# One sum of FFN weights out of four per pair: by VectorE from SBUF instead of a load and an adding transfer

## The chip, the cores and the metric

The kernel runs on one core of a Trainium2 chip. The metric is the device time of one execution in microseconds. TensorE (PE in the profile) does the matrix products, VectorE (DVE) and ScalarE (ACT) the elementwise work, GpSimd (POOL) some small copies and the issue of the adding transfers, SyncE (SP) the issue of the plain loads.

## What is computed

One inference step of a decoder of two layers, for a prompt of 512 tokens and for 8 samples of 4 tokens (544 columns together), all in fp32, with 1024 channels. Layer 0 mixes with attention and a gated linear attention, layer 1 with a short convolution. Each layer ends with the same feed-forward block, and the change touches that block alone:

```python
def causal_dwconv(x, past, w):
    L = x.shape[1]
    xp = jnp.concatenate([past.astype(x.dtype), x], axis=1)
    y = w[0] * xp[:, 0:L]
    for i in range(1, CONV_W):
        y = y + w[i] * xp[:, i:i + L]
    return y, xp[:, L:]
...
def conv_ffn(h, w_up, conv_w, conv_b, w_down, past):
    u = h @ w_up
    uc, new = causal_dwconv(u, past, conv_w)
    gate, val = jnp.split(uc + conv_b, 2, axis=-1)
    return (jax.nn.gelu(gate, approximate=True) * val) @ w_down, new
```

`w_up` is 1024 x 5632 (2816 gate and 2816 value columns, 22 blocks of 128 each), `w_down` 2816 x 1024.

## The kernel before

**Units.** Weights go through the kernel in units of 128 partitions x 512 columns of fp32 (256 KB). A load puts a unit into a raw tile `wr` (11 buffers). `prepare` (line 193) then makes two tiles of it: `wh`, the unit rounded for TensorE, on ScalarE (line 199), and `wl`, the rest, on VectorE (line 203). The units of the whole program stand in one list, and `prepare` goes through it in order: the `wh` stand in that order on ScalarE ("hi"), the `wl` on VectorE ("lo"), the loads on SP's queue ("load"), the adding transfers on GpSimd's queue ("sum"). `mm3` (line 276) makes each product of three matmuls: high weights with high activations (line 280), with low ones (line 285), and low weights with high ones (line 287).

**The FFN.** `ffn_order` (line 453) mixes three kinds of step per layer: the first gate and value blocks one by one ("raw", "plain"), then 16 pairs (one gate block and its value block, `c` = 6 to 21), and "down" steps between them. The pairs come in groups of 3, 4, 4 and 5, with a down step behind each; behind the last five there are two.

**A pair.** `pair(c)` (line 1800) makes a gate block and a value block by a scheme with 7 products where the plain way takes 8. Each product is 4 units' columns by 272 tokens: 12 matmuls. The weights that it needs, in order: `a`, `s2`, `s1`, `b`, `s3`, `s4`, `d`. Of these `a`, `b`, `d` are plain weights and the other four are sums: `s1` of the gate's and the value's blocks, `s2` = `s1` plus `a`'s block, `s3` of two blocks, and `s4` = `s2` plus `b`'s block. `quads` (line 244) makes the sums in flight: one plain load, and an adding transfer on top of it, either from HBM (`rows`, line 256) or from another tile in SBUF (`more`, line 252). So a pair has 7 loads on SP and 4 adding transfers on GpSimd. All seven tiles are taken when the first is prepared; a product asks for its units 8 units ahead (line 344), about one pair.

**The results of a pair** lie in four PSUM banks out of five of `pg`. They are emptied by ScalarE (lines 1807, 1811, 1813) and VectorE: line 1809 (`u2`) must be through before the bank's next product, two products after its own; 1815 (`u3`), 1818 and 1819 (gate), 1822 to 1824 (value) follow. `conv` (line 1737) then makes the convolution (1741 ACT, 1742 and 1743 DVE), 1750 the product of gate and value, 527 its low part. GpSimd copies the edge rows of each block (line 1739) and opens the next `u` (1714, 1715). A down step empties 16 banks into `m` (line 607).

**Order.** The code is written product by product, and a scheduler sets each engine's order from its own model of time, within the chains named above. Each engine then runs strictly in that order.

Of the kernel before, what the change touches and what calls it, by code (L numbers as in the profile page):

```python
# [16 lines left out]
ALU = mybir.AluOpType  # L17
AX = mybir.AxisListType

P = 128  # L20
# [68 lines left out]
def tile_hybrid_step(  # L89
# [42 lines left out]
    V, S, G, PE = nc.vector, nc.scalar, nc.gpsimd, nc.tensor  # L132
# [12 lines left out]
    def nm(s):  # L145
        uid[0] += 1
        return f"{s}{uid[0]}"
# [42 lines left out]
    def raw_tile():  # L190
        return wpool.tile([P, UN], F32, tag="wr", name=nm("wr"), bufs=11)
# [23 lines left out]
    def in_turn(what, ins):  # L215

        if what in turn:
            behind(ins, turn[what])
        turn[what] = ins

    def unit(w, r0, c0, nkb=4):


        def load():
            wr = raw_tile()
            ins = nc.sync.dma_start(
                wr.rearrange("p (k c) -> p k c", k=nkb),
                w[r0 : r0 + nkb * P, c0 : c0 + UN // nkb].rearrange("(k p) c -> p k c", p=P),
            )
            in_turn("load", ins)  # L230
            return wr

        return load
# [10 lines left out]
    def quads(w, c1, c2):  # L244

        t = {}

        def load(k, r0, c0):
            t[k] = unit(w, r0, c0)()

        def more(k, src):
            in_turn("sum", G.dma_start(t[k], src, accum_op=ALU.add))  # L252

        def rows(k, r0, c0):
            src = w[r0 : r0 + 4 * P, c0 : c0 + P].rearrange("(k p) c -> p k c", p=P)
            in_turn("sum", G.dma_start(t[k].rearrange("p (k c) -> p k c", k=4), src, accum_op=ALU.add))  # L256

        def first():
            load("a", 0, c1)
            load("s1", 0, c2)  # L260
            rows("s1", 4 * P, c2)
            load("s2", 0, c1)
            more("s2", t["s1"])
            load("b", 4 * P, c1)
            load("s3", 0, c1)
            rows("s3", 0, c2)
            load("s4", 4 * P, c1)
            more("s4", t["s2"])
            load("d", 4 * P, c2)
            return t["a"]  # L270

        return [first] + [lambda k=k: t[k] for k in ("s2", "s1", "b", "s3", "s4", "d")]

    nxt = [0]

# [15 lines left out]
    def behind(ins, first):  # L291

        tc.add_manual_dep(
            ins.ins,
            first.ins.name,
            mybir.DependencyInfo(mybir.DependencyClass.NoSync, mybir.DependencyReason.DATA),
            reason="issue order",
        )
# [166 lines left out]
    def ffn_units(l):  # L465
        for kind, c, n in ffn_order():
            if kind == "down":
                units.extend(down(ffn_down[l], c * P, n))
            elif kind != "pair":
                for k in range(c, c + n):  # L470
                    units.extend(cols(ffn_up[l], k * P) + cols(ffn_up[l], F + k * P))
            else:
                units.extend(quads(ffn_up[l], c * P, F + c * P))
# [1559 lines left out]
```

## Time and profile before

| what | value |
|---|---|
| median of 3 runs | 1285.26 us (1282.33 to 1285.63) |
| profiled execution, its own time | 1285.74 us |
| its span from the first to the last instruction | 1283.9 us |
| PE busy | 1241.9 us, 97% |
| DVE busy | 959.5 us, 75% |
| ACT busy | 682.9 us, 53% |
| POOL busy | 383.1 us, 30% |
| plain loads (q1) / adding transfers and other GpSimd transfers (q0) | 132.17 MB / 34.74 MB |

The profile is of one execution. Busy time says how long an engine had an instruction running; the stretches (windows of 20 us and the like) tell where it was not. The granted clock of TensorE is given as a share of full speed, 1.00 being 2.4 GHz.

### The profile page before, as it was taken

To read this page: it belongs to the slowest core of one execution; us is meant where nothing else is said; L and a number is where in the kernel's file an instruction comes from. 1 tells how busy PE (TensorE), PEld (TensorE's weight loads), DVE (VectorE), ACT (ScalarE), POOL (GpSimd) and SP (SyncE) were. 2 spreads that over 40 slices of the span, in tenths; PEclk is the share of its full clock that TensorE was granted. 3 is DMA by queue.
4 is the path that set the end of the run, shared out by engine and by line. 5 is a ranking of instruction groups with operands and counts; after the bars stand their busy time and mean duration, and the time that the engine had idled before them with its cause. 6 is when DMAs were issued, how large, how long until landed. Compare 5 with 4: busy or idle time off the path is not lost.

```text
span 1283.9 us, 26460 instructions
## 1 busy us (share of the span) xinstructions
PE 1241.9 (97%) x9710; PEld 1204.6 (94%) x9710; DVE 959.5 (75%) x2054; ACT 682.9 (53%) x1489; POOL 383.1 (30%) x604
## 2 busy tenths in 40 slices
PE   8999998989999999999998999999999999999997
PEld 7999986888999999999998999998999999999897
DVE  7486477578979796977978655528897969697786
ACT  7554546755567373735645323335556646464553
POOL 4100210063443334343144000025243433242312
PEclk9999999999999999999999999999999999999999
DMA  8512220323568999999622322321467899999811
GB/s 256 137 50 66 84 87 1 102 67 99 115 134 203 196 212 195 213 195 216 172 75 58 107 85 84 96 75 42 124 128 161 189 210 210 206 208 192 197 41 70
DMA packets 311883, 171.97 MB, mean 134 GB/s; under 512 B 20829, under 2 KB 301882, under 8 KB 311738
## 3 DMA queue, kind: packets, MB, share of 16 engines
q1 hardware_dynamic: 262914, 132.17, 36.0%
q0 software_dynamic: 43456, 34.74, 18.8%
q10 hardware_dynamic: 5384, 3.38, 0.9%
q8 instruction: 76, 1.25, 0.4%
q14 instruction: 53, 0.43, 0.1%
HBM read 149.01 MB, written 5.47 MB: 120 GB/s over the span
## 4 chain that ended last, share of the span: by engine, by line
PE 81%; DVE 11%; ACT 3%; issue 2%; DMA 2%; POOL 0%; SPq 0%; POOLq 0%; DVEq 0%; ACTq 0%
PE pg L280 24%; PE pg L285 24%; PE pg L287 24%; DVE m L652 3%; DVE xres L656 2%; DVE xl L668 2%; PE ps L181 1%; DVE wl L203 1%; PE ps L1088 1%; PE ps L1363 1%; DMA wr<-ffn_up 1%; ACT h L538 1%; PE ps L1425 1%; PE ps L390 1%; DVE xl L527 1%
## 5 line engine op out<-in xcount | busy, mean ns | idle before, releaser
L199 ACT ACTIVATE wh<-wr 128x512 fp32r<-128x512 f32 x478 | 296.8, 629 | 400.5 <-PE pg L285 322.8
L280 PE MATMUL pg<-xh,wh 128*128 128x256 f32 (+2 forms) x1536 | 445.3, 292 | 10.2 <-DVE u L1819 6.0
L285 PE MATMUL pg<-xl,wh 128*128 128x256 f32 (+2 forms) x1536 | 442.6, 290 | 0.3 <-DVE xl L530 0.3
L287 PE MATMUL pg<-xh,wl 128*128 128x256 f32 (+2 forms) x1520 | 437.0, 290 | 0.0
L203 DVE TENSOR_TENSOR wl<-wr,wh 128x512 fp32r<-128x512 f32 x466 | 318.3, 693 | 128.3 <-ACT wh L199 116.8
L280 PEld LDWEIGHTS pg<-xh,wh 128*128 128x128 f32 x1536 | 290.3, 190 | 14.7 <-issue 8.5
L285 PEld LDWEIGHTS pg<-xl,wh 128*128 128x128 f32 x1536 | 291.7, 190 | 1.0 <-DVE xl L530 0.5
L287 PEld LDWEIGHTS pg<-xh,wl 128*128 128x128 f32 x1520 | 287.6, 190 | 0.5 <-issue 0.2
L285 PE MATMUL pg<-gl,wh 128*128 128x256 f32 (+1 forms) x704 | 201.0, 288 | 0.8 <-DVE gl L527 0.8
L287 PE MATMUL pg<-gh,wl 128*128 128x256 f32 (+1 forms) x704 | 200.1, 288 | 0.0
L280 PE MATMUL pg<-gh,wh 128*128 128x256 f32 (+1 forms) x704 | 197.2, 290 | 2.1 <-DVE m L607 1.7
L285 PEld LDWEIGHTS pg<-gl,wh 128*128 128x128 f32 x704 | 132.6, 188 | 1.2 <-DVE gl L527 1.2
L280 PEld LDWEIGHTS pg<-gh,wh 128*128 128x128 f32 x704 | 129.8, 188 | 3.2 <-DVE m L607 2.3
L287 PEld LDWEIGHTS pg<-gh,wl 128*128 128x128 f32 x704 | 132.3, 188 | 0.0
L256 POOL DMA_DIRECT2D wr<-ffn_up x64 | 92.6, 1446 | 113.1 <-DVE wl L203 52.5
L252 POOL DMA_DIRECT2D wr<-wr x64 | 59.2, 925 | 210.7 <-DMA wr<-ffn_up 44.7
L607 DVE TENSOR_TENSOR m<-m,pg 128x256 f32<-128x256 f32 (+1 forms) x176 | 72.0, 432 | 55.4 <-PE pg L287 55.0
L280 PE MATMUL pg<-qh,wh 128*128 128x272 f32 x384 | 110.2, 289 | 0.6 <-DVE h L1809 0.6
L287 PE MATMUL pg<-qh,wl 128*128 128x272 f32 x384 | 110.7, 289 | 0.0
L285 PE MATMUL pg<-ql,wh 128*128 128x272 f32 x384 | 110.6, 288 | 0.0
L1739 POOL COPY uc<-u 128x18 f32<-128x18 f32 x88 | 63.9, 894 | 80.7 <-DVE u L1819 37.4
L539 POOL TENSOR_TENSOR pss<-pss,h 128x256 f32<-128x256 f32 (+1 forms) x47 | 38.5, 818 | 120.9 <-ACT h L538 120.3
(327 smaller groups left out, 2203.0 us busy)
## 6 DMA issues: line engine op xcount, KB each, us to landing
wr<-ffn_up SPq DMA_DIRECT2D x272, 256.0 KB, 3.6
wr<-ffn_down SPq DMA_DIRECT2D x88, 256.0 KB, 3.4
wr<-ffn_up POOLq DMA_DIRECT2D x64, 256.0 KB, 5.9
wr<-wr POOLq DMA_DIRECT2D x64, 256.0 KB, 4.6
wr<-w_in_odd SPq DMA_DIRECT2D x48, 256.0 KB, 2.9
wr<-w_in_even SPq DMA_DIRECT2D x28, 256.0 KB, 4.2
wr<-w_out_odd SPq DMA_DIRECT2D x16, 256.0 KB, 2.5
xt<-x_prompt SPq DMA_DIRECT2D x8, 256.0 KB, 3.4
```

The lines of the kernel that those rows point to most:

```text
L199: ins = S.activation(wh, src, AF.Copy)
L203: ins = eng.tensor_tensor(wl, src, wh.bitcast(F32), ALU.subtract)
L252: in_turn("sum", G.dma_start(t[k], src, accum_op=ALU.add))
L256: in_turn("sum", G.dma_start(t[k].rearrange("p (k c) -> p k c", k=4), src, accum_op=ALU.add))
L280: ins = PE.matmul(ps[:, :n], lhsT=wh, rhs=xh[kb][:, sl], start=first, stop=False, skip_group_check=True)
L285: PE.matmul(ps[:, :n], lhsT=wh, rhs=xl[kb][:, sl], start=False, stop=last and packed, skip_group_check=True)
L287: PE.matmul(ps[:, :n], lhsT=wl, rhs=xh[kb][:, sl], start=False, stop=last, skip_group_check=True)
L539: ins = (V if c == NC - 1 else G).tensor_tensor(ss[:, sl], ss[:, sl], q[:, :n], ALU.add)
L607: V.tensor_tensor(self.m[m][:, sl], self.m[m][:, sl], ps[:, :n], ALU.add)
L652: chain(V.scalar_tensor_tensor(m, m, gcol(self.kind, self.l, c), self.bc[:, sl], ALU.mult, ALU.mult))
L656: chain(V.tensor_tensor(x, x, self.m[c][:, sl], ALU.add))
L1739: G.tensor_copy(ucv[:, :, :, c], u[:, TP : TP + 54].rearrange("p (g k) -> p g k", k=6)[:, :, 0:2])
```

## The change

`s4` is no longer loaded and added to in flight. When its turn comes, `last_sum` takes a raw tile and VectorE writes `b` + `s2` into it from the tiles in SBUF (line 272 of the changed kernel), in the chain "lo" of the `wl`. The other three sums stay.

```diff
             load("b", 4 * P, c1)
             load("s3", 0, c1)
             rows("s3", 0, c2)
-            load("s4", 4 * P, c1)
-            more("s4", t["s2"])
             load("d", 4 * P, c2)
             return t["a"]
 
-        return [first] + [lambda k=k: t[k] for k in ("s2", "s1", "b", "s3", "s4", "d")]
+        def last_sum():
+            wr = raw_tile()
+            in_turn("lo", V.tensor_tensor(wr, t["b"], t["s2"], ALU.add))
+            return wr
+
+        return [first] + [lambda k=k: t[k] for k in ("s2", "s1", "b", "s3")] + [last_sum, lambda: t["d"]]
```

With 16 pairs in each of two layers, 32 loads and 32 adding transfers go (SP's queue has 480 rows instead of 512, GpSimd 566 instead of 598) and 32 instructions come to VectorE (2021 instead of 1989). The scheduler sets the order anew around them; line numbers behind line 272 are 3 higher.

**GpSimd, the last two pairs of layer 0, before.** The tiles 8003, 8006, 8011, 8014 are `s1`, `s2`, `s3`, `s4` of pair 20, and 8175, 8178 `s1`, `s2` of pair 21.

```order
L256 DMA wr_8011<-ffn_up 128x4x128
L252 DMA wr_8014<-wr_8006 128x512
L256 DMA wr_8175<-ffn_up 128x4x128
L252 DMA wr_8178<-wr_8175 128x512
L1739 COPY uc_3682<-u_7889 128x18
L1739 COPY uc_3682<-u_7886 128x18
```

The same place of the changed kernel: 7997 is `s3` of pair 20, 8160 and 8163 are `s1` and `s2` of pair 21, and `u_8041`, `u_8044` belong to pair 19.

```order
L256 DMA wr_7997<-ffn_up 128x4x128
L1717 MEMSET u_8041 128x2
L1718 COPY u_8041<-stT_3138 128x8x2
L1717 MEMSET u_8044 128x2
L1718 COPY u_8044<-stT_3138 128x8x2
L256 DMA wr_8160<-ffn_up 128x4x128
L1742 COPY uc_3682<-u_8041 128x18
L1742 COPY uc_3682<-u_8044 128x18
L1717 MEMSET u_8212 128x2
L1718 COPY u_8212<-stT_3138 128x8x2
L1717 MEMSET u_8215 128x2
L1718 COPY u_8215<-stT_3138 128x8x2
```

The adding transfer into `s4` of pair 20 no longer stands ahead of `s1` of pair 21; that into `s2` of pair 21 (the row behind these) has moved behind the copies of pair 19's edge rows.

**VectorE, the same place, before.** `wl_8236` is the low part of `s2` of pair 21, `u_8058` and `u_8061` are gate and value of pair 19.

```order
L1815 TENSOR_TENSOR h_8057<-pg_8051,h_8054 128x272
L203 TENSOR_TENSOR wl_8236<-wr_8178,wh_8237 128x512
L1818 TENSOR_TENSOR u_8058<-pg_8052,h_8056 128x240
L1819 TENSOR_TENSOR u_8058<-pg_8052,h_8056 128x8x4
L1822 TENSOR_TENSOR u_8061<-h_8057,h_8055 128x240
L1823 TENSOR_TENSOR u_8061<-h_8057,h_8055 128x8x4
```

And of the changed kernel, where the low part of `s2` of pair 21 is `wl_8218`, and gate and value of pair 19 are `u_8041` and `u_8044`.

```order
L1827 TENSOR_TENSOR u_8044<-h_8040,pg_8036 128x272
L203 TENSOR_TENSOR wl_8117<-wr_8115,wh_8118 128x512
L203 TENSOR_TENSOR wl_8134<-wr_8000,wh_8135 128x512
L203 TENSOR_TENSOR wl_8173<-wr_8158,wh_8174 128x512
L1745 SCALAR_TENSOR_TENSOR y_8153<-u_8041,cw_3121,y_8153 128x560
L1812 TENSOR_TENSOR h_8210<-h_8208,pg_8205 128x272
L1745 SCALAR_TENSOR_TENSOR y_8193<-u_8044,cw_3121,y_8193 128x560
L1746 SCALAR_TENSOR_TENSOR y_8153<-u_8041,cw_3121,y_8153 128x560
L1746 SCALAR_TENSOR_TENSOR y_8193<-u_8044,cw_3121,y_8193 128x560
L1753 TENSOR_TENSOR y_8153<-y_8153,y_8193 128x560
L203 TENSOR_TENSOR wl_8218<-wr_8163,wh_8219 128x512
L203 TENSOR_TENSOR wl_8235<-wr_8160,wh_8236 128x512
```

The low part of `s2` of pair 21 has moved from ahead of the emptying of pair 19's banks to ten rows behind it.

**VectorE in a down step, changed kernel,** between groups of four pairs: the sum of the next group's first pair (`wr_5764`) stands between the emptyings of the down banks (line 610, before line 607).

```order
L610 TENSOR_TENSOR m_3674<-m_3674,pg_5548 128x288
L203 TENSOR_TENSOR wl_5760<-wr_5613,wh_5761 128x512
L272 TENSOR_TENSOR wr_5764<-wr_5611,wr_5608 128x512
L610 TENSOR_TENSOR m_3675<-m_3675,pg_5575 128x256
L610 TENSOR_TENSOR m_3675<-m_3675,pg_5576 128x288
```

Before, the same place has no sum.

```order
L607 TENSOR_TENSOR m_3674<-m_3674,pg_5551 128x288
L203 TENSOR_TENSOR wl_5766<-wr_5616,wh_5767 128x512
L607 TENSOR_TENSOR m_3675<-m_3675,pg_5578 128x256
L607 TENSOR_TENSOR m_3675<-m_3675,pg_5579 128x288
```

Of a group of four pairs, the sums of the first and the second stand in the down step ahead or right behind it, those of the third and fourth among the pairs.

## Rows read from the trace of the kernel before

**Rows 1.** Page, part 1: busy us, share of the span, instructions.

```profile
PE 1241.9 (97%) x9710; PEld 1204.6 (94%) x9710; DVE 959.5 (75%) x2054; ACT 682.9 (53%) x1489; POOL 383.1 (30%) x604
```

**Rows 2.** Stretches: start:end, us, PE, PEld, DVE, ACT, POOL busy, clock, DMA share, GB/s.

```profile
580.00:600.00 20.00, 20.00 (x162) 20.00 (x161) 18.26 (x37) 13.61 (x26) 6.59 (x11) 1.00 1.00 212
600.00:620.00 20.00, 17.18 (x125) 16.99 (x124) 13.42 (x27) 10.80 (x22) 5.05 (x15) 0.91 0.83 196
...
1200.00:1220.00 20.00, 16.85 (x120) 16.45 (x120) 14.94 (x30) 11.53 (x23) 6.71 (x15) 0.91 0.85 196
```

**Rows 3.** Chain that ended last, layer 0's last pairs: start us, us, what.

```profile
609.73 0.90 issue
...
612.54 0.50 PE pg L280
613.04 0.23 PE pg L285
...
616.44 0.12 PE pg L285
```

**Rows 4.** Timeline of ACT and DVE there: start, us, engine, line, operation, [idle before].

```profile
610.63 1.67 ACT L199 ACTIVATE wh<-wr 128x512 fp32r<-128x512 f32 x3 [7.09 <-PE pg L287]
...
611.29 0.69 DVE L203 TENSOR_TENSOR wl<-wr,wh 128x512 fp32r<-128x512 f32 x1 [6.36 <-ACT wh L199]
```

**Rows 5.** Timeline of POOL ahead of it, and one row of layer 1.

```profile
594.49 0.89 POOL L252 DMA_DIRECT2D wr<-wr  x1 [1.77 <-DVE wl L203]
595.20 1.52 POOL L256 DMA_DIRECT2D wr<-ffn_up  x1
603.12 0.88 POOL L252 DMA_DIRECT2D wr<-wr  x1 [6.40 <-DVE wl L203]
603.67 0.69 POOL L1739 COPY uc<-u 128x18 f32<-128x18 f32 x2
...
1203.67 2.34 POOL L1739 COPY uc<-u 128x18 f32<-128x18 f32 x2
```

**Rows 6.** DMA from 440 to 620 us: queues (packets, MB, share), issues (us to landing).

```profile
q1 hardware_dynamic: 50038, 25.36, 49.8%
q0 software_dynamic: 14256, 11.27, 44.5%
...
wr<-ffn_up POOLq DMA_DIRECT2D x21, 256.0 KB, 6.1
wr<-wr POOLq DMA_DIRECT2D x21, 256.0 KB, 4.7
```

**Rows 7.** Waits of SP's queue from 440 to 620 us: total, times, longest.

```profile
SPq L226 <- DMA wr<-wr: 42.1, 7, 10.5
```

**Rows 8.** Stretches of four pairs and of the down step behind them: DVE alone.

```profile
446.70:485.40 38.70, 35.32 (x72) 1.00 0.93 217
485.40:508.50 23.10, 16.43 (x32) 1.00 0.94 186
```

**Rows 9.** Timeline of DVE: a down step, and low parts back to back.

```profile
433.38 0.84 DVE L607 TENSOR_TENSOR m<-m,pg 128x256 f32<-128x256 f32 x2 [1.39 <-PE pg L287]
...
595.29 1.29 DVE L203 TENSOR_TENSOR wl<-wr,wh 128x512 fp32r<-128x512 f32 x2
```

**Rows 10.** Timeline of DVE: line 1809 in the four pairs from 442 us.

```profile
442.83 0.44 DVE L1809 TENSOR_TENSOR h<-h,pg 128x272 f32<-128x272 f32 x1 [0.29 <-PE pg L287]
...
465.63 0.43 DVE L1809 TENSOR_TENSOR h<-h,pg 128x272 f32<-128x272 f32 x1
```

**Rows 11.** Timeline of DVE at the end of these four pairs.

```profile
485.48 0.69 DVE L203 TENSOR_TENSOR wl<-wr,wh 128x512 fp32r<-128x512 f32 x1 [1.85 <-ACT wh L199]
486.23 1.55 DVE L1742 SCALAR_TENSOR_TENSOR y<-u,cw,y 128x560 f32<-128x560 f32 x2
...
489.12 1.48 DVE L607 TENSOR_TENSOR m<-m,pg 128x256 f32<-128x256 f32 x4
```

**Rows 12.** Chain that ended last at the same place.

```profile
489.20 0.34 DVE m L607
```

## The prediction

> **What bounds the kernel now.** I read the busy times first: TensorE has work for 97% of the span, VectorE for 75% [rows 1]. So only what takes idle time out of TensorE can gain, and an engine at 75% on average can still be full where it matters. Next the stretches of 20 us, to find where TensorE is not full: in undisturbed ones it runs 162 matmuls, 0.1235 us each, and in all the FFN there are two large holes, at the end of the last five pairs of either layer, with 125 and 120 matmuls and a granted clock of 0.91 [rows 2]. Small ones lie at the ends of the other groups of pairs. Then the chain at the first hole: TensorE ends a product at 609.7, starts the next at 612.54, and runs its matmuls at 0.23 us apart until 616, when they are 0.12 again [rows 3]; before it fell to that lower level (1.2 GHz against 2.4) it had been idle for the hole. What it waited for: ScalarE had sat idle for 7.09 us until it could round a unit, VectorE for 6.36 us behind that, with the emptying of a full bank queued behind this low part [rows 4]. By the order, the unit is `s2` of pair 21. Its sum was issued by GpSimd at 603.12, after a wait of 6.40 us for the adding transfer into `s1`, which itself had been issued at 595.20 [rows 5]. So the hole hangs on GpSimd's chain of adding transfers, beside DMA queues that are 94% taken from 440 to 620 us, 44.5 points by the adding queue although it moves less than half of the other's bytes [rows 6].
>
> **What goes.** Per pair one load and one of four adding transfers. In the stretch of rows 6 there are 42 adding transfers for 44.5 points, so a quarter of them gives back some 11 points, and ten loads of 256 KB, 2.6 MB of the plain queue's 25.36, some 5 more: the queues fall from 94% to about 78%. SP's queue waited 42.1 us in 7 waits on adding transfers that still read a tile [rows 7]; `d`'s buffer no longer waits for one that reads `s2`. On GpSimd the issue of the sum into `s4` goes: in the trace it waited 1.77 us and took 0.89 us ahead of the issue into `s1` of pair 21 [rows 5], which could have stood at 592.7 instead of 595.2. That alone brings the `s2` behind it 2.5 us forward. The transfers take 6.1 and 4.7 us from issue to landing [rows 6]; with queues at 78% I take each a microsecond shorter. So `s2` would be there some 4.5 us earlier, against a hole of 2.8 us [rows 3].
>
> The worth of the hole: TensorE is 162 - 125 = 37 matmuls short in layer 0 and 42 in layer 1, at 0.1235 us 4.6 and 5.2 us, 9.8 us together [rows 2]. From the other side: 20 - 17.18 and 20 - 16.85 us of idle are 6.0 us, and some 14 matmuls at 0.23 in place of 0.125 us in each hole are 1.5 us each [rows 3]: 9.0 us. I take 9.0, since a few matmul records may be missing.
>
> **What is added.** 32 sums on VectorE of 128x512. No row shows an addition of two raw tiles. The nearest is the low part, the same size from two tiles in SBUF: 0.69 us alone, two of them in 1.29 us [rows 4, 9], so 0.60 us of VectorE's time each when one follows another. 32 times 0.60 to 0.69 is 19 to 22 us, and the question is what hides it. The wait for data is nothing new, as `b` and `s2` have had their own low parts made ahead in the chain "lo". Behind the sum, ScalarE's rounding waits for VectorE and VectorE's low part for ScalarE; the order puts other rows between.
> - *In the down steps* VectorE is idle 1.39 us out of 3 behind each pair of emptied banks [rows 9], and 6.7 us of 23.1 in all [rows 8]. Of four sums of a group, two stand there or at its end: free.
> - *Among the pairs* VectorE is at 35.3 of 38.7 us [rows 8]; the other two sums (three in the groups of five) bring 1.2 to 1.4 us into 3.4 us of idle time, 1.85 us of which is itself a wait for a sum [rows 11]. Whether TensorE notices depends on line 1809: it has the two products between, 24 matmuls or 2.96 us. In the four pairs from 442 us it runs when TensorE lets it, at 442.83, and in the third pair at 465.63 [rows 10], where two pairs of 84 matmuls (10.4 us each) would put it at 463.6: 2.0 us late. In the new order I count VectorE's rows between two such lines: between the second and the third pair 7 low parts and a sum, between the third and the fourth 9 and a sum. With 0.60 to 0.65 us for these, 0.75 us for each step of the convolution [rows 11] and the rest as in the trace, that is some 9.5 and 13 us against 10.4 each: up to 2 us late, inside 2.96. I count nothing.
> - *At the group ends* TensorE waits 0.34 us today for `m` [rows 12], because VectorE comes late out of the pairs. The sums make it later by 1.2 us, the wait of 1.85 us for a sum [rows 11] goes. Six such ends (three per layer) can give from -0.5 us (today's stall gone) to +0.7 us (a sum exposed) each: -3 to +4 us. I take 0.
>
> **The sum.** The profiled execution took 1285.74 us, 1283.9 of it span; 1285.74 - 9.0 + 0 = 1276.7. The median of the runs is 0.5 us below that execution: 1276.3 us. Bounds of this case: -9.8 - 3 gives 1272.5, -9.0 + 4 with a microsecond of the hole left 1281.
>
> **Rivals.**
> *The wait stays on GpSimd.* The first three sums still go one after the other through its queue, and in the new order the issue into `s2` of pair 21 has moved behind the copies of pair 19's edge rows, which wait until VectorE has emptied pair 19's banks. From there: two copies, 0.7 us, four small ones, 0.6 us, issue and landing 4.7 us, 0.63 us for the rounding, nearly 7 us after pair 19's end; TensorE needs the unit one pair and one product after it, 11.9 us. That speaks against this rival; for it speaks that landing varies and that the copies wait for a late VectorE. It would keep the holes or half of them: 1281.5 to 1286, I say 1284.
> *GpSimd is held up by the new instructions.* The copy pair took 0.69 us once and 2.34 us in layer 1, where VectorE was running low parts [rows 5]. If the copies of two pairs ahead of `s2` stretch like that (twice 1.65 us) and VectorE is 2 us late besides, the margin of 4.9 us is used up, and a hole of up to 2 us without a fall of the clock stays in each layer: 1280. The Trainium skill says in "SBUF — State Buffer", section "SBUF: two separate sides", that VectorE and GpSimd share a pair of ports, which an instruction of VectorE with two inputs in SBUF holds against one of GpSimd that reads SBUF, for its whole length; the two copy rows agree with that. By it the time would be that of this rival, without it that of the forecast.
> *VectorE becomes the bound,* the case that ends slower. Place: line 1809 and the emptying into `m`. Price: the sums among the pairs, 9 or so per layer, each exposed at 0.65 us, 11.7 us, and the low parts come so late that the holes stay: 1297; with the holes gone 1288. It decides from the point where line 1809 is more than 2.96 us late. For it: 2.0 us are used today, and the pairs leave 3.4 us in 38.7. Against it: two sums of four stand outside the pairs.
> *The change doesn't do what it says:* excluded, the row counts of SP, GpSimd and VectorE change by 32 each.
>
> **How the numbers follow.** The forecast has 0.57, the wait on GpSimd 0.24, GpSimd held up 0.05, VectorE as the bound 0.14. A measurement of this kernel tells some 0.3% from no change, 3.9 us: faster is below 1281.4, slower above 1289.1. The forecast (1272.5 to 1281) and the held-up GpSimd are faster: 0.62. The wait on GpSimd is the same, and a small part of VectorE as the bound: 0.26. The rest, 0.12, is slower. The range from 1272 to 1287 holds the first three cases and leaves out VectorE as the bound and a little at the lower end.
>
> **What would show it.** If right: in the stretches at 600 and 1200 us of the new trace TensorE has about 162 matmuls and a clock of 1.00; DMA share among the pairs near 0.8; VectorE near 980 us busy; adding transfers land in under 4.5 us; no wait of ScalarE over 3 us on a sum. If the chain shows line 272, `h` of line 1812 or `m` of line 610 ahead of TensorE for more than a microsecond in several groups, VectorE has become the bound. If ScalarE still waits 5 us or more at the end of the five pairs, the wait has stayed on GpSimd. The prediction is wrong above all if the scheduler's new order was made from times that the chip does not keep.

## The result, and the profile after

The changed kernel takes 1321.4 us (median of 4 runs, 1316.2 to 1325.61) where the kernel before took 1285.45 beside it (4 runs, 1282.33 to 1289.81): a ratio of 1.0267, 95% interval 1.0240 to 1.0294. It is slower by some 34 us; the forecast was faster by 9, and the range ended at 1287. The profiled execution took 1316.2 us, 1314.4 of it span.

The page, part 1 and part 3 (queue: packets, MB, share of 16 engines), against [rows 1] and the table of the time before:

```profile
PE 1248.7 (95%) x9710; PEld 1210.7 (92%) x9710; DVE 979.6 (75%) x2086; ACT 682.7 (52%) x1489; POOL 372.6 (28%) x572
...
q1 hardware_dynamic: 246018, 123.78, 32.5%
q0 software_dynamic: 38848, 26.35, 14.4%
```

All that the change was counted to move has moved: 32 more instructions on VectorE and 20.1 us more of busy time, 32 fewer on GpSimd, 8.4 MB less in either queue. TensorE has the same 9710 matmuls and more idle time. Where, the stretches of 20 us tell (columns as in [rows 2]); first those with the holes of layer 0, then the two places where the holes of before were:

```profile
420.00:440.00 20.00, 16.35 (x108) 16.35 (x109) 14.97 (x31) 7.45 (x13) 5.41 (x9) 0.83 0.64 121
480.00:500.00 20.00, 16.11 (x127) 15.62 (x126) 16.21 (x32) 10.42 (x21) 10.04 (x17) 1.00 0.92 204
560.00:580.00 20.00, 16.54 (x109) 16.13 (x108) 14.64 (x32) 6.50 (x12) 6.38 (x11) 0.83 0.79 159
640.00:660.00 20.00, 17.22 (x126) 16.74 (x125) 20.00 (x43) 10.67 (x26) 1.72 (x4) 0.91 0.65 185
...
600.00:620.00 20.00, 20.00 (x162) 20.00 (x162) 16.56 (x31) 12.64 (x25) 10.59 (x16) 1.00 0.90 173
1200.00:1220.00 20.00, 20.00 (x162) 20.00 (x161) 13.25 (x25) 8.14 (x16) 4.33 (x9) 1.00 0.53 122
```

The stretches at 600 and 1200 us are full, but they now hold an earlier part of the program. There is a hole at the end of every group of pairs, in layer 0 and in layer 1 alike, where before only the last group of a layer had a large one. The four above lack 54, 35, 53 and 36 of 162 matmuls, 178 in all, 22 us by 0.1235 us each; in layer 1 the stretches from 1020, 1040, 1100, 1180 and 1260 us lack 34, 16, 45, 46 and 21, 162 in all. Less the 37 and 42 of the two holes of before, that is 261 matmuls, 32 us, about the 30.5 us by which the two profiled spans differ. So the new holes, with the lower clock in three of the four stretches above (0.83 and 0.91), are the loss.

The waits of the engines (waiting line, what released it: us in total, times, longest) name the road that leads there:

```profile
PE pg L283 <- ACT gh L529: 22.6, 6, 4.0
PE pg L283 <- DVE m L610: 7.2, 5, 1.9
ACT wh L199 <- DMA wr<-wr: 47.9, 18, 7.5
POOL uc L1742 <- DVE u L1826: 173.2, 20, 16.6
SPq L226 <- DVE wr L272: 57.0, 23, 5.4
```

TensorE waits for `gh` at the ends of the first three groups of each layer, 3.4 to 4.0 us each time. In ScalarE's order this `gh` stands behind the `wh` of a sum that is late (ScalarE's waits for such sums before: 9.0 us in 5, none over 3.7). GpSimd waits for VectorE ahead of its copies of edge rows. And the last row is new: SP's queue, which issues the plain loads, waits for the new sum. The hole at the end of the last group is of another kind: TensorE waits there for `m` of line 610 (1.86 us at 646.74, 1.70 us in layer 1), and VectorE is busy for all 20 us of the stretch at 640. These two holes, 36 and 21 matmuls, are 7 of the 32 us.

Followed in order of time, one hole of the larger kind (the timelines of VectorE, SP, GpSimd, ScalarE and TensorE at the end of the third group; start, us, engine, line, operation, [idle before]):

```profile
534.98 0.69 DVE L272 TENSOR_TENSOR wr<-wr,wr 128x512 f32<-128x512 f32 x1
...
547.87 0.68 DVE L272 TENSOR_TENSOR wr<-wr,wr 128x512 f32<-128x512 f32 x1
...
535.73 13.22 SPq L226 DMA_DIRECT2D wr<-ffn_down  x8
...
548.58 0.37 SPq L226 DMA_DIRECT2D wr<-ffn_down  x1
...
549.00 0.50 SPq L226 DMA_DIRECT2D wr<-ffn_up  x1
...
551.47 0.98 SPq L226 DMA_DIRECT2D wr<-ffn_up  x2
...
552.97 0.28 PE L283 MATMUL pg<-gh,wh 128*128 128x256 f32 x1
...
554.86 1.30 POOL L256 DMA_DIRECT2D wr<-ffn_up  x1 [3.36 <-DVE y L1745]
...
559.80 0.29 PE L283 MATMUL pg<-gh,wh 128*128 128x288 f32 x1
...
561.63 0.90 POOL L252 DMA_DIRECT2D wr<-wr  x1 [5.47 <-DMA wr<-ffn_up]
...
565.89 0.63 ACT L199 ACTIVATE wh<-wr 128x512 fp32r<-128x512 f32 x1 [6.87 <-DMA wr<-wr]
566.43 0.73 ACT L529 ACTIVATE gh<-y 128x512 fp32r<-128x512 f32 x2
...
567.10 0.58 PE L283 MATMUL pg<-gh,wh 128*128 128x256 f32 x1 [3.43 <-ACT gh L529]
```

The sum of the last pair but one ends at 535.67, and SP issues the first load of the down step's weights at 535.73. The sum of the last pair ends at 548.55, and SP issues the eighth of these loads at 548.58. Only behind it, in SP's fixed order, come the loads of the next pair: `a` at 549.00 and, after another wait for a low part of VectorE's, `s1` at 551.47. From there everything waits for the step before it: `s1` lands, its adding transfer is issued at 554.86, the one into `s2` at 561.63, and ScalarE rounds `s2` at 565.89. Behind that stands the last `gh` that the down step needs (that of the last pair but one), and TensorE starts again at 567.10. In the kernel before the same loads stood at (SP's timeline there, then ScalarE's):

```profile
520.87 14.27 SPq L226 DMA_DIRECT2D wr<-ffn_down  x8
...
535.24 1.61 SPq L226 DMA_DIRECT2D wr<-ffn_up  x3
...
548.02 0.73 ACT L526 ACTIVATE gh<-y 128x512 fp32r<-128x512 f32 x2
551.92 0.63 ACT L199 ACTIVATE wh<-wr 128x512 fp32r<-128x512 f32 x1 [3.16 <-issue]
```

They were some 14 us earlier, but so was the whole program: the group's first product starts at 506.27 there and at 516.61 after. Measured from it, `a` comes at 29.0 us before and at 32.4 us after. What counts is how far the next group's first load runs ahead of the down step. TensorE's first matmul of that step stands at 548.42 before and at 552.97 after, which gives 13.2 and 4.0 us. But TensorE's order differs: after, a few matmuls of the down step stand ahead of the last products of the last pair, and TensorE stays in the step only from 559.80 on; before, it does so from 548.42. Measured to that point, the **lead** was 13.2 us and now is 10.8 us. It can be read at each group's end in the same way and is used below.

ScalarE's order differs too, as the last two rows show: before, the down step's last `gh` stood ahead of the rounding of the next pair's `s2`, so that a late `s2` did not hold it up.

Why the loads hang on the sum is in the code and in the times. Eleven raw tiles are used over and over, and a load has to wait until the tile that it takes has been read. A pair asks for seven. Which load takes which tile is not on record; counted eleven requests back, the first load of the down step takes the place of `b` of the last pair but one, the eighth that of `b` of the last pair, and these two are issued 0.06 and 0.03 us behind the end of a sum. Before, `b` was free when its low part was made. The sum reads `b` and `s2` at `s4`'s turn, two units after `b`'s in the list, and keeps `b` until then.

### The profile page after: what moved, and what is told of

Its sections match the earlier page's. It is cut to its first block, busy times and chain, and to the rows that moved or that the text cites. A ratio compares the mean times of both kernels' runs of the same rounds, so it can differ in the third digit from the quotient of the medians.

```text
span 1314.4 us, 26211 instructions
## 1 busy us (share of the span) xinstructions
PE 1248.7 (95%) x9710; PEld 1210.7 (92%) x9710; DVE 979.6 (75%) x2086; ACT 682.7 (52%) x1489; POOL 372.6 (28%) x572
## 3 DMA queue, kind: packets, MB, share of 16 engines
q0 software_dynamic: 38848, 26.35, 14.4%
## 5 line engine op out<-in xcount | busy, mean ns | idle before, releaser
L199 ACT ACTIVATE wh<-wr 128x512 fp32r<-128x512 f32 x478 | 288.3, 627 | 379.3 <-PE pg L288 268.4
L283 PE MATMUL pg<-gh,wh 128*128 128x256 f32 (+1 forms) x704 | 203.2, 300 | 28.8 <-ACT gh L529 22.6
L288 PE MATMUL pg<-gl,wh 128*128 128x256 f32 (+1 forms) x704 | 206.6, 296 | 0.8 <-DVE gl L530 0.8
L290 PE MATMUL pg<-gh,wl 128*128 128x256 f32 (+1 forms) x704 | 204.9, 295 | 0.0
L288 PEld LDWEIGHTS pg<-gl,wh 128*128 128x128 f32 x704 | 138.1, 196 | 1.2 <-DVE gl L530 1.2
L290 PEld LDWEIGHTS pg<-gh,wl 128*128 128x128 f32 x704 | 137.4, 196 | 0.0
L1742 POOL COPY uc<-u 128x18 f32<-128x18 f32 x88 | 43.2, 531 | 289.2 <-DVE u L1826 173.2
L256 POOL DMA_DIRECT2D wr<-ffn_up x64 | 104.2, 1651 | 58.9 <-DVE wl L203 17.0
L1718 POOL COPY u<-stT 128x16 f32<-128x16 f32 x88 | 91.9, 1252 | 11.4 <-ACT stT L1672 11.4
L1744 ACT ACTIVATE y<-u,cw 128x560 f32<-128x560 f32 x88 | 73.2, 848 | 29.6 <-DVE u L1822 25.0
```

Source lines behind the costliest of these rows:

```text
L199: ins = S.activation(wh, src, AF.Copy)
L283: ins = PE.matmul(ps[:, :n], lhsT=wh, rhs=xh[kb][:, sl], start=first, stop=False, skip_group_check=True)
L288: PE.matmul(ps[:, :n], lhsT=wh, rhs=xl[kb][:, sl], start=False, stop=last and packed, skip_group_check=True)
L290: PE.matmul(ps[:, :n], lhsT=wl, rhs=xh[kb][:, sl], start=False, stop=last, skip_group_check=True)
L1718: G.tensor_copy(smp(u)[:, :, 0:2], stv[:, :, :, c])
L1742: G.tensor_copy(ucv[:, :, :, c], u[:, TP : TP + 54].rearrange("p (g k) -> p g k", k=6)[:, :, 0:2])
```

## The experiments

Four theories were put against each other. **1:** in the new order GpSimd's adding transfers stand behind copies of edge rows that wait for VectorE. **2:** the 32 sums take VectorE's time. **3:** `gh` stands behind `wh` on ScalarE. **4:** the sum holds raw tiles longer, and the loads come late. Theory 4 was found only after the first four runs. All ratios are to the kernel before on the same chip, with a 95% interval.

The scheduler sets the orders anew for each edit. Counted in the traces, some 1% at most of VectorE's and ScalarE's rows change places where the copies move in the changed kernel and where tiles are held without time. In the others that were counted (copies earlier or on ScalarE in the kernel before, whole dead sums at either place, and the three kernels with the sum in another tile or place) 6 to 12% of VectorE's rows do, so that the edit is not the only difference there.

### GpSimd's order

**The copies one pair later**, in the changed kernel; `put_edges` makes the copies of the pair before, behind the last adding transfer issued so far:

```diff
         def conv(c):
             u = us[c]
-            G.tensor_copy(ucv[:, :, :, c], u[:, TP : TP + 54].rearrange("p (g k) -> p g k", k=6)[:, :, 0:2])
+            edges.append((c, u))
...
             product(pa, xq["11"], True)
+            put_edges()
```

> The changed kernel, but GpSimd's edge-row copies of a pair are put into its order one pair later, so that s1, s2 and s3 of the pair after next stand ahead of them. Theory 1 (the slowdown is GpSimd's new order: the adding transfers stand behind copies that wait for VectorE): 1270 to 1290 us, and the idle time of ScalarE before `wh` on `wr<-wr` falls from 48 us to under 20. Theory 2 (VectorE's 32 extra sums delay the emptying of the banks): 1312 to 1325, as the changed kernel. Theory 3 (the `gh` of a group's last pair stands behind the next group's `wh` in ScalarE's order): no change either unless the sums land in time; then 1285 or less.

Measured: 1308.96 us, ratio 1.0149 (1.0125 to 1.0174). That is between the ranges of theories 1 and 2, and ScalarE's waits for a sum fall to 25.5 us, not under 20.

**The copies on ScalarE**, in the changed kernel, so that GpSimd has nothing of the kind left among the pairs:

```diff
-            G.tensor_copy(ucv[:, :, :, c], u[:, TP : TP + 54].rearrange("p (g k) -> p g k", k=6)[:, :, 0:2])
+            edge = u[:, TP : TP + 54].rearrange("p (g k) -> p g k", k=6)[:, :, 0:2]
+            if c % FC < PLAIN:
+                G.tensor_copy(ucv[:, :, :, c], edge)
+            else:
+                S.activation(ucv[:, :, :, c], edge, AF.Copy)
```

> The changed kernel with the 64 edge-row copies of the pairs on ScalarE, right ahead of the convolution's instruction that reads the same `u` and so waits for the same VectorE work; on GpSimd nothing but the opening of the next `u` is left among the adding transfers. Theory 1: 1270 to 1288 us, no ScalarE wait over 3 us on a sum. Theory 2: 1312 to 1325. Theory 3: between, 1290 to 1310, with TensorE still waiting for `gh` at the group ends.

Measured: 1308.92 us, ratio 1.0152 (1.0129 to 1.0176). Both give the same: 1.2 of the 2.7 per cent come back, more than half of the loss stays. The timelines of SP, GpSimd, ScalarE at the same group's end of the second kernel show why:

```profile
550.60 12.36 SPq L226 DMA_DIRECT2D wr<-ffn_up  x11
...
556.93 1.30 POOL L256 DMA_DIRECT2D wr<-ffn_up  x1 [17.89 <-DVE h L1816]
563.75 0.90 POOL L252 DMA_DIRECT2D wr<-wr  x1 [5.52 <-DVE u L1826]
...
568.09 0.63 ACT L199 ACTIVATE wh<-wr 128x512 fp32r<-128x512 f32 x1 [6.31 <-DMA wr<-wr]
```

GpSimd stands idle for 17.89 us with no copy ahead, until the next pair's `s1`, loaded late, is there. So theory 1 is not the root; these runs led to theory 4. The time is within what theory 3 expected here, and TensorE waits for `gh` as in the changed kernel, 22.7 us in 6 waits: that `gh` stands behind `wh`, as it did not before, is the last link of the road. The order of the two was not changed by itself, so what it costs alone is not shown; the runs below close the holes by bringing the loads earlier, with that order kept.

**The copies earlier, in the kernel before:** a copy takes its place in the chain of the adding transfers, as it stands in the code.

```diff
+            ins = G.tensor_copy(ucv[:, :, :, c], u[:, TP : TP + 54].rearrange("p (g k) -> p g k", k=6)[:, :, 0:2])
+            if c % FC >= PLAIN:
+                in_turn("sum", ins)
```

> The kernel before, but the edge-row copies of the pairs join the chain of the adding transfers on GpSimd, so that the copies of a pair stand ahead of all the sums of the pair after next that are written behind it; VectorE's work is that of before. Theory 1: slower, 1300 to 1330 us, with holes at the ends of the groups. Theory 2: 1282 to 1290, as before.

Measured: 1364.06 us, ratio 1.0579 (1.0557 to 1.0602). ScalarE's waits there:

```profile
ACT wh L199 <- DMA wr<-wr: 153.0, 46, 8.1
```

So copies ahead of the adding transfers can cost far more than theory 1 expected: the mechanism is real. The 75 us are those of the edit with the new orders of all engines (12% of VectorE's rows stand elsewhere), not of the copies alone. Whether the order of before costs anything, the copies on ScalarE tell in the kernel before:

> The kernel before with the pairs' 64 edge-row copies on ScalarE. If copies ahead of adding transfers cost only where the loads are late already: 1286 to 1291 us, as before. If they make the two holes at the ends of the five-pair groups of the kernel before: 1276 to 1282.

Measured: 1292.99 us, ratio 1.0024 (0.9995 to 1.0054): nothing gained, 2 us above the range for that case. The two holes of before are not made by the copies.

### VectorE's time and the held tiles, in the kernel before

**32 whole dead sums** at the place of the changed kernel's own, all four sums still made in flight:

```diff
+        def dead_sum():
+            in_turn("lo", V.tensor_tensor(t["b"], t["b"], t["s2"], ALU.add))
+            return t["s4"]
...
+        return [first] + [lambda k=k: t[k] for k in ("s2", "s1", "b", "s3")] + [dead_sum, lambda: t["d"]]
```

> The kernel before with 32 more additions on VectorE at the place where the changed kernel has its own (`b` + `s2`, written over `b` after its last use); all four sums are still made in flight. Theory 2: slower by as much as the changed kernel, 1310 to 1325 us. Theory 1: the scheduler moves some copies ahead of an adding transfer here too, but by less: 1285 to 1300.

Measured: 1312.31 us, ratio 1.0176 (1.0147 to 1.0206), in the range of theory 2; but this edit both takes VectorE's time and holds `b` and `s2`. The next two take these apart. **Hold without time** (the same on 8 of 512 columns):

```diff
+            in_turn("lo", V.tensor_tensor(t["b"][:, 0:8], t["b"][:, 0:8], t["s2"][:, 0:8], ALU.add))
```

> The kernel before with a token addition on VectorE where the changed kernel has its sum: 8 of 512 columns of `b` + `s2`, written over `b` after its last use. It costs next to no VectorE time but keeps the raw tiles of `b` and `s2` until `s4`'s turn, as the sum does. Theory 4 (the sum holds `b` and `s2` two units longer, the eleven raw tiles rotate, and the loads behind them on SP come late): 1305 to 1315 us, as with the 32 whole dead sums (1312). Theory 2 (the time of the sums on VectorE): 1283 to 1292, as before.

Measured: 1303.35 us, ratio 1.0108 (1.0079 to 1.0137); VectorE's busy time is 962.2 us, 2.7 more than before. That is 2 us under the range of theory 4 and well above that of theory 2. So some 14 us come from holding tiles for two units, with next to no time of VectorE's and nearly the orders of before. They come by another road than the holes of the change: TensorE waits 11.5 us in 6 for `m` (5.0 in 5 before) and never for `gh`. **Time with next to no hold** (`b` + `b` over `b`, right behind `b`'s low part):

```diff
+            in_turn("lo", V.tensor_tensor(t["b"], t["b"], t["b"], ALU.add))
+            return t["s3"]
```

> The kernel before with 32 dead whole additions on VectorE (`b` + `b` over `b`) right behind `b`'s low part: VectorE's time of the sums without a longer hold of `s2` and with 0.7 us more of `b`. Theory 2 with the part that the dead sums and the token sums left between them (1312 against 1303): 1294 to 1300 us. Theory 4 alone, VectorE's time hidden: 1286 to 1292.

Measured: 1304.0 us, ratio 1.0098 (1.0067 to 1.0129), above both ranges. So the edit that adds VectorE's time has a price too where the queues are as full as before, some 13 us. Here also SP is found waiting for the added instruction, and TensorE for `gh` (waits of SP's queue and of TensorE):

```profile
SPq L226 <- DVE wr L273: 57.5, 23, 4.1
...
PE pg L284 <- ACT gh L530: 9.6, 4, 3.6
```

The lead, at 13.5 and 12.6 us at the second and third group, is near that of before (13.3 and 13.2), but ScalarE's new order has `gh` behind the `wh` of `s2`, as in the changed kernel. In the kernel with the hold alone `gh` stands ahead of it, and TensorE does not wait for it. So the 13 us may be the price of that order as much as of VectorE's time.

> The kernel before with the 32 dead whole additions behind `b`'s low part (1304 us by themselves) and the pairs' edge-row copies on ScalarE (1293 by themselves). If VectorE's additions cost time through the copies that wait for VectorE ahead of the adding transfers: 1290 to 1296. If they cost it in another way (later low parts, later free raw tiles, GpSimd's other instructions): 1301 to 1308.

The two edits together. Measured: 1305.79 us, ratio 1.0118 (1.0101 to 1.0135): the 13 us do not go through the copies. Late low parts that free raw tiles late would fit the first row above, the order of `gh` and `wh` the second; neither was isolated.

### Six tiles or seven, late or early

The test of theory 4 in the changed kernel itself: the same 32 whole sums on VectorE, the same loads and transfers, only another tile and another place. **In place** (the sum over `s2`; six tiles per pair, `b` still held):

```diff
         def last_sum():
-            wr = raw_tile()
-            in_turn("lo", V.tensor_tensor(wr, t["b"], t["s2"], ALU.add))
-            return wr
+            in_turn("lo", V.tensor_tensor(t["s2"], t["b"], t["s2"], ALU.add))
+            return t["s2"]
```

> The changed kernel with the sum written over `s2` instead of into a raw tile of its own, at the same place: six raw tiles per pair instead of seven; `s2` stays until `s4` is used, `b` until the sum. VectorE's work is that of the changed kernel. Theory 4: 1275 to 1292 us, most of the loss gone. Theory 2: 1310 to 1325.

Measured: 1281.52 us, ratio 0.9935 (0.9916 to 0.9955).

**In place and early** (right behind `b`'s low part; nothing held longer than before):

```diff
+        def sum_early():
+            in_turn("lo", V.tensor_tensor(t["s2"], t["b"], t["s2"], ALU.add))
+            return t["s3"]
...
+        return [first] + [lambda k=k: t[k] for k in ("s2", "s1", "b")] + [sum_early, lambda: t["s2"], lambda: t["d"]]
```

> As the kernel with the sum over `s2`, but the sum is made right behind `b`'s low part, one place earlier in the list than `s3`'s, so that `b`'s raw tile is free at once and nothing stays longer than in the kernel before. Theory 4: 1270 to 1285 us, no slower than the in-place sum at the old place. Theory 2: 1310 to 1325.

Measured: 1274.77 us, ratio 0.9883 (0.9860 to 0.9905): faster than both kernels.

**Early, in a tile of its own** (`t["s4"] = raw_tile()` as the target):

> The sum right behind `b`'s low part, but into a raw tile of its own: seven raw tiles per pair as in the changed kernel, `b` free at once as in the early in-place kernel. Together with the changed kernel (seven tiles, late: 1321), the in-place sum at the old place (six, late: 1282) and the early in-place sum (six, early: 1275) it makes four cases of two questions. If the longer hold of `b` and `s2` is what costs: 1275 to 1290 us. If the seventh tile, taken from the rotation at the sum's turn, is what costs: 1300 to 1325.

Measured: 1285.75 us, ratio 0.9967 (0.9945 to 0.9989).

| ratio to before | seven tiles per pair | six |
|---|---|---|
| sum at `s4`'s turn | 1.0267 (the change) | 0.9935 |
| sum behind `b`'s low part | 0.9967 | 0.9883 |

Either edit alone takes back all of the loss. Both bring the loads earlier. The copies still wait for VectorE ahead of adding transfers in both kernels with seven tiles (241 us for `u` of two lines in the change, 185 in the other). The lead, worked out as above at the ends of the first three groups of layer 0, and beside it the time from the load to the first matmul of the down step:

| kernel | lead, us | to the first matmul, us | ratio |
|---|---|---|---|
| before | 16.7, 13.3, 13.2 | 13.0, 13.3, 13.2 | 1 |
| the change | 12.1, 10.9, 10.8 | 8.4, 4.1, 4.0 | 1.0267 |
| its copies on ScalarE | 12.1, 11.8, 12.0 | 8.4, 5.0, 5.1 | 1.0152 |
| in place | 15.0, 14.6, 14.6 | 11.7, 11.1, 11.1 | 0.9935 |
| early, own tile | 14.5, 14.4, 14.2 | 14.5, 10.6, 10.4 | 0.9967 |
| in place and early | 16.4, 15.2, 15.2 | 13.0, 12.1, 12.1 | 0.9883 |

At the second and third group the lead puts these six kernels in the order of their times. The lateness is not all: the kernel before with tiles held (hold without time) has leads of 15.8, 11.3 and 11.8 us and loses only 1.1%, with `gh` ahead of `wh` as in the kernel before.

In the early in-place kernel, SP's and ScalarE's timelines at the third group's end and the stretches of the old holes:

```profile
521.06 12.38 SPq L226 DMA_DIRECT2D wr<-ffn_down  x8
535.42 14.30 SPq L226 DMA_DIRECT2D wr<-ffn_up  x11
...
551.59 0.63 ACT L199 ACTIVATE wh<-wr 128x512 fp32r<-128x512 f32 x1 [1.76 <-DMA wr<-wr]
552.13 0.73 ACT L528 ACTIVATE gh<-y 128x512 fp32r<-128x512 f32 x2
...
600.00:620.00 20.00, 20.00 (x162) 20.00 (x161) 19.19 (x39) 13.89 (x29) 7.00 (x15) 1.00 0.75 191
1200.00:1220.00 20.00, 20.00 (x162) 20.00 (x162) 18.38 (x39) 14.93 (x30) 4.25 (x12) 1.00 0.48 118
```

The loads are back where they were (521, 535), and the holes of [rows 2] are gone. `gh` stands behind the `wh` of `s2` here too, as in the changed kernel, but `s2` is rounded 1.0 us after TensorE's unbroken down step begins (550.62), where in the change it was 6.1 us.

### What is left of the other causes, and more of the same

**The early in-place kernel without VectorE's time** (8 of 512 columns of the sum):

> The early in-place kernel with only 8 of 512 columns of each sum added (the rest of `s4` is left out, so its products are wrong): the raw tiles, loads and transfers of the early in-place kernel without VectorE's time of the sums. If VectorE's sums are hidden once the loads come in time, as the prediction had it: 1271 to 1277 us, as the whole sums (1275). If they cost here what the dead ones cost in the kernel before (13 us): 1260 to 1265.

Measured: 1273.53 us, ratio 0.9865 (0.9851 to 0.9880), against 0.9883 (0.9860 to 0.9905) with the whole sums: a difference of 2 us, with intervals that overlap. With the loads in time, VectorE's sums are hidden to within these 2 us.

**With the copies on ScalarE besides:**

> The in-place early sum, and the 64 edge-row copies of the pairs on ScalarE instead of GpSimd. Theory 4 with theory 1 (both the raw tiles and the copies ahead of the adding transfers cost): 1265 to 1280 us, below the early sum alone. Theory 4 alone: as the early sum alone within 3 us. Theory 2: 1305 to 1320.

Measured: 1276.15 us, ratio 0.9890 (0.9868 to 0.9912): no difference. With the loads in time, the copies cost nothing.

**A second sum on VectorE** (`s1` + `a` over `a`):

```diff
-            load("s2", 0, c1)
-            more("s2", t["s1"])
...
+        def sum_first():
+            in_turn("lo", V.tensor_tensor(t["a"], t["a"], t["s1"], ALU.add))
+            t["s2"] = t["a"]
+            return t["s2"]
```

> The early in-place sum, and `s2` too made by VectorE (`s1` + `a`, over `a`, right behind `a`'s low part), so that five raw tiles, five loads and two adding transfers per pair are left. Theory 4 (raw tiles and late loads set the time): 1262 to 1276 us. If VectorE, with another 19 to 22 us of sums, has become the bound: 1278 to 1295.

Measured: 1289.31 us, ratio 0.9995 (0.9976 to 1.0013). The first expectation missed: the gain of the first sum is used up. Most of it goes in one stretch of each layer, at the first pair, and in the first of these ScalarE has this wait:

```profile
360.00:380.00 20.00, 17.59 (x126) 17.35 (x126) 15.54 (x31) 9.44 (x25) 8.91 (x3) 0.91 0.43 91
960.00:980.00 20.00, 17.66 (x126) 17.25 (x126) 15.51 (x32) 9.31 (x24) 9.16 (x3) 0.91 0.45 92
...
367.21 1.15 ACT L199 ACTIVATE wh<-wr 128x512 fp32r<-128x512 f32 x2 [4.95 <-DVE wr L273]
```

ScalarE waits 4.95 us for the second sum, which stands at 366.44 on VectorE, behind other work without idle time from 357.72 on. That fits the second expectation, VectorE as the bound, at this one place; at the ends of the second and third groups TensorE is full (160 and 162 matmuls in the stretches from 480 and 540 us). Whether VectorE's time or the place of the sum in its order costs this was not taken apart.

## Why the prediction was wrong, point by point

**The step that failed** is in "What is added": "The wait for data is nothing new, as `b` and `s2` have had their own low parts made ahead". That is true of the sum, and it was where the question ended. What was not asked is who waits for the tiles that the sum reads. SP was looked at only for what goes (the 42.1 us of [rows 7] and `d`'s tile), not for what comes: 57.0 us of waits for line 272. The missing term is the lead of the loads, which the sum put at nothing: 13.2 us down to 10.8 at the third group. With `gh` behind `wh` in ScalarE's new order it makes holes of 3.4 to 4.0 us at six of the eight groups' ends. In the text it would have been one more step: `b` stays until `s4`'s turn, two units on; the down step's first and eighth load wait for tiles that a sum has held; SP issues in order, so the next pair's `s1` moves with them. The sum of SP's waits alone would not have told it. In the early in-place kernel, which loses nothing, it is nearly the same:

```profile
SPq L226 <- DVE wr L271: 54.7, 32, 3.0
```

**What goes** was right, and its size on the low side. The early in-place kernel has the same transfers as the change and no longer hold. It is some 15 us faster than the kernel before beside it, where the forecast had 9.0. Both holes are closed at a clock of 1.00 there. Adding transfers between tiles land in 3.8 us in it and in 4.2 us in the changed kernel (under 4.5 was forecast, 4.7 in [rows 6]). So the reason given for the two holes of before, the chain of adding transfers on full queues, fits, though the chain and the full queues were not taken apart; that moving the copies gains nothing there is measured (1.0024, 0.9995 to 1.0054).

**VectorE's sums at nothing** was right in size and wrong as to when. Their busy time is as forecast (979.6 for 980). They are hidden in the early in-place kernel, to within some 2 us. In the kernel before, with no transfer taken away, the edit that adds the same time costs 13 us, with `gh` moved behind `wh` by the new order. The rival with VectorE as the bound had a price of 11.7 us for that. Its mark, a wait of over a microsecond for `m` of line 610, is there after the change at the end of the last group of each layer (1.86 and 1.70 us; these holes are 7 of the 32 us). The larger part of TensorE's new waits, 22.6 us, is for `gh`, and all of these holes go in the early in-place kernel with VectorE's work unchanged.

**The wait stays on GpSimd** named as its mark a wait of ScalarE of 5 us or more at the end of the five pairs. There it has become short: under 3 us, where before it was 7.09 us [rows 4] and 5.91 us in layer 1. So the chain that the prediction followed did shorten. Waits of 6.9 to 7.5 us for a sum stand at the ends of the second and third groups instead. The copies ahead of the adding transfers have a part in them: moving them gives 1.2 of 2.7 per cent; with loads in time it gives nothing. The price of 1284 assumed that only the old holes could stay; that new ones arise at every group's end was in no case.

**GpSimd held up by new instructions:** the mechanism is there, but the new sums are not seen to add to it. One copy that opens a `u` in the changed kernel, and the instruction of VectorE beside it:

```profile
541.06 1.80 POOL L1718 COPY u<-stT 128x16 f32<-128x16 f32 x1
...
542.01 0.80 DVE L1745 SCALAR_TENSOR_TENSOR y<-u,cw,y 128x560 f32<-128x560 f32 x1
```

The copy ends at 542.86, VectorE's instruction with two inputs in SBUF at 542.81. Of the 176 small copies of this kernel 106 take over 0.4 us, and 82 of these end within 0.15 us behind such an instruction; the shortest take 0.2 us. That agrees with the rule of the Trainium skill that the prediction quotes, in "SBUF — State Buffer", section "SBUF: two separate sides". In the page's groups (line, out<-in xcount | busy, mean ns of one | idle before), though, these copies take no longer with the whole sums than with 8 columns of them:

```profile
L1717 POOL COPY u<-stT 128x16 f32<-128x16 f32 x88 | 68.0, 889 | 11.5 <-ACT stT L1671 11.5
...
L1717 POOL COPY u<-stT 128x16 f32<-128x16 f32 x88 | 75.3, 986 | 11.5 <-ACT stT L1671 11.5
```

The first is the early in-place kernel, the second the one with 8 columns. In the change itself they take 1252 ns, 715 before, while the edge-row copies fall from 894 to 531; what that costs was not measured by itself.

**The order.** "The prediction is wrong above all if the scheduler's new order was made from times that the chip does not keep" named a part of it: the new order has copies ahead of adding transfers and `gh` behind a late `wh`. But with that order on ScalarE kept and a tile's life shortened, which the code sets, the holes close. What the order costs by itself was not measured; that holes at `gh` arise with the tiles hardly held (1.0098) says that it is not nothing.

## What to carry to other kernels

Where an operation moves from a queue to an engine, ask for each operand not only when it is there but until when it is now held, and which load takes its buffer next; with buffers used over and over and loads issued in order, two units of longer hold cost 1.1% by themselves. Put such an operation right behind the last other use of its operand and write over an operand that is dead: the same sum then gave 1.2% instead of costing 2.7%. Measure the lead of the loads (first load of the next group against the point from which TensorE stays in the step before it) before and after; at the second and third group it put six kernels in the order of their times, where busy times and bytes did not. And look what stands in the same engine's order behind the instruction that waits for a late load.

## What was not expected

32 whole additions cost 13 us or next to nothing, depending on the rest of the kernel and on the order that the scheduler sets around them: 0.7 to 1.3% with the queues as before (94% taken among the pairs), some 0.2% where a quarter of the adding transfers is gone. And the edit that moves 64 copies of 18 columns ahead of adding transfers in GpSimd's queue costs 75 us, more than any change of VectorE's or the queues' load in these runs.
